# Cross-covariance attention on one core: one late store cut as 68 and 60 partitions, and all work in a new order

## The chip, the cores and the metric

The kernel runs on one core of a Trainium2 chip. The metric is the device time of one execution in microseconds; the other cores are idle. Beside it stands the span, the time from the first to the last instruction of the program in a profiled execution.

## The reference

```
Q, K, V: [8, 12, 512, 64] float32
Q_norm = Q / (norm(Q, axis=-2) + 1e-10)          # over the 512 positions
K_norm = K / (norm(K, axis=-2) + 1e-10)
attn = einsum('bhnd,bhne->bhde', Q_norm, K_norm)  # 64 x 64 for each head
attn = softmax(attn, axis=-1)                     # + 1e-10 under the line
out  = einsum('bhnd,bhde->bhne', V, attn)         # float32
```

There are 96 heads. Each of Q, K, V and the output is 12.58 MB.

## The kernel before, in words

The 96 heads are taken in twelve groups of eight, `s` = 0 to 11. Heads lie along partitions: a group's Q is one tile of 128 partitions by 2 x 1024 elements, 1 MB, and K is another. V comes in twelve loads of 1 MB, two for each pair of groups (`w` = 0 to 5); a group's output leaves as one store of 1 MB. So the program moves 48 times 1 MB: 24 loads of Q and K, 12 loads of V, 12 stores. The tiles of group 0 alone come in halves. Each 1 MB of Q, K or output consists of 256 rows of 4096 bytes, each row one DMA packet.

For a group: `cast_qk` makes bf16 copies of Q and K, `square` squares both, `grams` multiplies K by Q for each head (64 matmuls), `sums` adds the squares over the positions (8 matmuls), `fold`, `norms` and `powers` make the factors, `scale_k`, `logits`, `scales_q`, `exps` and `normalise` make the softmax. For a pair of groups `cast_v` casts V in four pieces, `vtrans` transposes it in four or five pieces, `vcopy` brings these out of PSUM. Then `outs` (16 matmuls) and `ocopy` run four times for each group, and `store` sends the group out.

Casts, squares and the copies out of PSUM may run on several engines. Which engine takes which piece, and the order of everything, is decided at build time by the planner `Order`: it steps through a list of pieces with costs (given where the pieces are added), ranks (`R`), preferences of engines (`BIAS`) and paces of the loads (`QK_PACE`, `V_FROM`, `V_PACE`, `ST_LAG`), always taking the piece that can begin first. The instructions are then emitted in that order, and each engine works through its own in order. So the constants in `PAR` fix the program.

All DMAs but two are issued by SyncE, in one queue. A DMA carries one of eight semaphores in turn, so it waits for the landing of the DMA eight before it; it waits too for its buffer. The numbers of buffers are in `PAR['NB']`: `qk` of Q and K tiles, `v` of V tiles, `sq` of squares, `so` of output tiles. `ocopy` of a group waits until the store that last used its `so` buffer has landed.

`store` sends a group in one DMA, except group 9 (`S - SPLIT`): it goes in two halves (`r` = 0, 1), each 128 rows of 4096 bytes, one a partition, and each half is cut along the partitions as `CUTS` says. Before, half 0 goes as partitions 0 to 85, 85 to 117 and 117 to 128, and half 1 whole. Groups 10 and 11 follow whole; they are the last two DMAs.

SyncE's order before (Q1 is the Q of group 1, V0 the first load of V, S0 the store of group 0):

```
Q0a Q0b | Q1 K1 V0 V1 Q2 K2 V2 Q3 K3 Q4 K4 V3 Q5 V4 K5 V5 Q6 K6 Q7 K7 V6 Q8 K8 V7 V8 Q9 K9
Q10 K10 V9 Q11 K11 S0 V10 V11 S1 S2 S3 S4 S5 S6 S7 S8 S9(85) S9(32) S9(11) S9(half 1) S10 S11
```

Of the kernel before, what the change touches and what calls it, by code (L numbers as in the profile page):

```python
# [10 lines left out]
AF = mybir.ActivationFunctionType  # L11
ALU = mybir.AluOpType

PAR = {'NB': {'qk': 7, 'v': 3, 'vb': 2, 'qm': 2, 'sq': 2, 'vt': 2, 'so': 6, 'sm': 2, 'ab': 4},
 'TAIL': 3,
 'FINE': (0,),
 'ACTQ': True,
 'X': 1.27,
 'R': {'ck': 14.3601,
       'q': -46.9145,  # L20
       'sq': -4.5261,
       'sk': 21.309,
       'gr': 31.9137,
       's1': -8.269,
       'rd': 14.1273,
       'nn': -13.565,
       'pw': -22.1669,
       'kx': 16.8281,
       'lg': -36.3133,
       'qs': 14.727,  # L30
       'ex': 7.4539,
       'nm': 23.5766,
       'cv': -5.1919,
       'vt': 13.5707,
       'vc': 31.4911,
       'ou': -17.6156,
       'oc': 6.4318},
 'BIAS': {('cv', 'DVE'): 12.3272,
          ('vc', 'ACT'): 5.2627,
          ('oc', 'DVE'): 7.9654,  # L40
          ('q0', 'ACT'): -9.0842,
          ('sk', 'ACT'): 4.174,
          ('sk', 'DVE'): 5.4091,
          ('cv', 'ACT'): 0.906,
          ('cv', 'POOL'): -0.1651,
          ('ck', 'DVE'): -11.8527,
          ('ck', 'ACT'): -10.4645,
          ('ck', 'POOL'): -15.4937,
          ('oc', 'ACT'): 4.7795,
          ('sq', 'DVE'): -12.3114,  # L50
          ('sq', 'ACT'): -21.9953,
          ('q0', 'DVE'): -28.6804,
          ('q0', 'POOL'): -29.3142,
          ('vc', 'DVE'): -20.4676},
 'QK_PACE': 0.9356,
 'V_FROM': 0.0874,
 'V_PACE': 0.7666,
 'ST_LAG': 6.0835,
 'SPLIT': 3,
 'CUTS': (((0, 85), (85, 117), (117, 128)), ((0, 128),))}  # L60

D = 64
T = 32
# [86 lines left out]
def kernel(  # L150
# [11 lines left out]
    W = S // 2  # L162
    TAIL = PAR["TAIL"]
    FINE = PAR["FINE"]

# [6 lines left out]

    NB = PAR["NB"]
    edge = ctx.enter_context(tc.tile_pool(name="edge", bufs=1))
# [25 lines left out]
    def cols(c):  # L200
        return slice(0, T) if c is None else slice(c * TT, (c + 1) * TT)
# [9 lines left out]
    def load_qk(s, x, c):  # L211
        w, e = divmod(s, 2)
        if (s, x) not in qk32:
            qk32[s, x] = qp.tile([128, T, D], F32, name="qk32")
        issue = nc.scalar if (s, x) == (0, 1) and PAR["ACTQ"] else nc.sync
        o = qk32[s, x][:, cols(c)].rearrange("p t d -> p (t d)")
# [10 lines left out]
    def store(s, i):  # L227
        if s == S - PAR["SPLIT"]:
            for r in range(2):
                o, y = Of[s // 2, s % 2, :, r], so[s][:, r].rearrange("p j d -> p (j d)")  # L230
                for a, b in PAR["CUTS"][r]:
                    nc.sync.dma_start(out=o[a:b], in_=y[a:b])
        elif i is None:
            nc.sync.dma_start(out=Of[s // 2, s % 2], in_=so[s].rearrange("p r j d -> p r (j d)"))
        else:
            nc.sync.dma_start(out=Of[s // 2, s % 2, :, i], in_=so[s][:, i].rearrange("p j d -> p (j d)"))
# [280 lines left out]
```

## Time and profile before

| | |
|---|---|
| time, median of 3 runs | 129.66 us (129.61 to 130.15) |
| time of the profiled execution | 129.72 us |
| its span | 127.6 us |
| bytes moved | 50.59 MB, 37.75 MB read and 12.58 MB written in HBM |
| busy: PE, DVE, ACT, POOL | 80.8, 80.4, 85.1, 47.0 us |
| granted TensorE clock, mean | 0.878 |

In the profile's rows PE is TensorE's matmuls, PEld its weight loads, DVE, ACT and POOL are VectorE, ScalarE and GpSimd; SPq is the queue of SyncE, which issues the DMAs. "DMA share" is the mean busy share of the core's 16 DMA engines; it can come out a little over 1. L12 is line 12 of the kernel. The profiled execution's time lies 2.1 us over its span.

### The profile page before, as it was taken

How to read it: one execution, taken by the hardware profiler on the slowest of the kernel's cores; microseconds unless marked ns; L12 is line 12 of the kernel's file. 1: busy time of each engine (PE TensorE's matmuls, PEld its weight loads, DVE VectorE, ACT ScalarE, POOL GpSimd, SP SyncE). 2: the span in 40 equal slices, each digit the busy share in tenths (PEclk: the TensorE clock that was granted, in tenths of full speed). 3: DMA queues.
4: the chain of work that ended last, by engine and by line, in shares of the span. 5: the costliest groups of instructions: out<-in, count | busy, mean ns of one | idle time of the engine just before them, and what ended most of it. 6: DMA issues, size and time to landing. Idle time of an engine off the chain costs nothing.

```text
span 127.6 us, 4062 instructions
## 1 busy us (share of the span) xinstructions
PE 80.8 (63%) x1800; PEld 54.0 (42%) x1800; DVE 80.4 (63%) x140; ACT 85.1 (67%) x116; POOL 47.0 (37%) x40
## 2 busy tenths in 40 slices
PE   0009459883797687676469897946999699950000
PEld 0006146560674365354336655532577267630000
DVE  2223344899836988889886699985699976600000
ACT  4076658794698826998798988839479757880000
POOL 3250665460545196054518805442516400000000
PEclk9999999999559999999976999995599967998555
DMA  4999999999999999999999999999999999999950
GB/s 117 412 419 437 421 414 437 408 420 416 429 420 429 419 420 408 421 415 428 407 434 415 416 419 420 428 414 416 430 419 416 414 417 414 415 416 406 408 234 15
DMA packets 11601, 50.59 MB, mean 396 GB/s; under 512 B 832, under 2 KB 832, under 8 KB 10048
## 3 DMA queue, kind: packets, MB, share of 16 engines
q1 hardware_dynamic: 11296, 49.29, 94.2%
q10 hardware_dynamic: 288, 1.05, 2.1%
q8 instruction: 14, 0.23, 0.6%
q14 instruction: 3, 0.02, 0.0%
HBM read 37.75 MB, written 12.58 MB: 394 GB/s over the span
## 4 chain that ended last, share of the span: by engine, by line
DMA 53%; PE 13%; DVE 12%; ACT 7%; SPq 4%; issue 2%
DMA qk<-in_Q_dram 36%; DMA v<-in_V_dram 17%; ACT so L205 4%; PE po L338 3%; SPq L225 3%; PE gram L289 3%; PE vps L323 3%; DVE ab L310 2%; PE l L266 2%; DVE vt L207 2%; PE gram L260 1%; DVE s L271 1%; ACT sq L251 1%; DVE sq L253 1%; ACT vb L205 1%
## 5 line engine op out<-in xcount | busy, mean ns | idle before, releaser
L209 POOL TENSOR_SCALAR kb<-qk 128x2048 bf16<-128x2048 f32 (+1 forms) x13 | 23.7, 1820 | 37.8 <-DMA qk<-in_K_dram 30.0
L251 ACT ACTIVATE sq<-qb 128x2048 bf16<-128x2048 bf16 (+1 forms) x13 | 23.1, 1778 | 8.2 <-DVE qb L207 8.2
L205 ACT COPY so<-po 128x512 f32<-128x512 f32 x47 | 25.6, 584 | 4.1 <-PE po L338 2.6
L209 POOL TENSOR_SCALAR vb<-v 128x1024 bf16<-128x1024 f32 x15 | 20.3, 1372 | 13.5 <-DMA v<-in_V_dram 9.8
L338 PE MATMUL po<-ab,vt 128*32 128x128 bf16 x768 | 20.6, 237 | 5.2 <-DVE ab L310 2.5
L260 PE MATMUL gram<-qb,kb 32*128 32x128 bf16 x768 | 15.3, 238 | 12.7 <-POOL kb L209 10.1
L323 PE MATMUL vps<-ident,vb 128*128 128x128 f32 x96 | 17.2, 304 | 4.9 <-POOL vb L209 2.7
L207 DVE CAST qb<-qk 128x2048 bf16<-128x2048 f32 (+1 forms) x12 | 13.6, 1137 | 10.3 <-DMA qk<-in_Q_dram 9.5
L266 PE MATMUL l<-sq,hm 128*32 128x512 bf16 x96 | 18.5, 446 | 2.1 <-ACT sq L251 1.5
L260 PEld LDWEIGHTS <-kb 32*128 32x128 bf16 x768 | 13.1, 104 | 14.8 <-POOL kb L209 11.4
L338 PEld LDWEIGHTS <-vt 128*32 128x32 bf16 x768 | 14.4, 103 | 11.2 <-issue 6.5
L207 DVE COPY vt<-vps 128x1024 bf16<-128x1024 bf16 (+1 forms) x25 | 16.5, 665 | 3.0 <-PE vps L323 2.7
L251 ACT ACTIVATE sq<-kb 128x2048 bf16<-128x2048 bf16 (+1 forms) x10 | 17.4, 1737 | 0.6 <-POOL kb L209 0.6
L205 ACT CAST vb<-v 128x1024 bf16<-128x1024 f32 x9 | 12.0, 1338 | 6.8 <-DMA v<-in_V_dram 6.8
L323 PEld LDWEIGHTS vps<-ident,vb 128*128 128x128 f32 x96 | 11.1, 151 | 8.7 <-POOL vb L209 3.3
L271 DVE TENSOR_REDUCE s<-l 64x128 f32<-64x512 f32 x12 | 8.1, 678 | 7.9 <-PE l L266 7.9
L289 PE MATMUL gram<-ident,kqs 128*128 128x128 f32 x48 | 9.7, 335 | 4.0 <-DVE kqs L285 3.7
L295 DVE TENSOR_TENSOR ls<-gram,r 64x256 f32<-64x256 f32 x24 | 10.1, 420 | 2.7 <-PE gram L289 2.3
L310 DVE TENSOR_TENSOR ab<-ex,rb 128x512 bf16<-128x512 f32 x12 | 10.4, 867 | 0.4
L285 DVE TENSOR_TENSOR kqs<-gram,r 128x512 f32<-128x512 f32 x12 | 8.3, 688 | 3.4 <-ACT r L281 2.9
L289 PEld LDWEIGHTS gram<-ident,kqs 128*128 128x128 f32 x48 | 6.2, 166 | 8.1 <-DVE kqs L285 7.3
L266 PEld LDWEIGHTS <-hm 128*32 128x32 bf16 x96 | 5.5, 104 | 9.4 <-issue 7.5
(25 smaller groups left out, 41.3 us busy)
## 6 DMA issues: line engine op xcount, KB each, us to landing
v<-in_V_dram SPq DMA_DIRECT2D x12, 1024.0 KB, 19.5
qk<-in_Q_dram SPq DMA_DIRECT2D x11, 1024.0 KB, 19.7
qk<-in_K_dram SPq DMA_DIRECT2D x11, 1024.0 KB, 19.7
out_dram<-so SPq DMA_DIRECT2D x11, 1024.0 KB, 15.3
qk<-in_K_dram ACTq DMA_DIRECT2D x2, 512.0 KB, 7.2
qk<-in_Q_dram SPq DMA_DIRECT2D x2, 512.0 KB, 5.8
out_dram<-so SPq DMA_DIRECT2D x1, 512.0 KB, 9.8
out_dram<-so SPq DMA_DIRECT2D x1, 340.0 KB
```

The source lines that it names most:

```text
L205: nc.scalar.copy(o, i)
L207: nc.vector.tensor_copy(o, i)
L209: nc.gpsimd.tensor_scalar(out=o, in0=i, scalar1=1.0, scalar2=0.0, op0=ALU.mult, op1=ALU.add)
L251: nc.scalar.activation(o, i, AF.Square)
L260: nc.tensor.matmul(gram[s][:, h, 0], k, q, start=(t == 0), stop=(t == TT - 1))
L266: nc.tensor.matmul(st[s][32 * x:32 * (x + 1)].rearrange("p t d -> p (t d)"), hm, sq[s][:, x, t:t + 4].rearrange("p t r d -> p (t r d)"), s ...
L271: nc.vector.tensor_reduce(out=s2[s], in_=st[s].rearrange("p t d -> p d t"), axis=mybir.AxisListType.X, op=ALU.add)
L289: nc.tensor.transpose(gram[s][:, h, 1], kqs[s][:, h], ident)
L295: nc.vector.tensor_tensor(out=ls[s][half], in0=gram[s][half, :, 1, half], in1=r12[s][half, :HU, None].to_broadcast([D, HU, D]), op=ALU.mult)
L310: nc.vector.tensor_tensor(out=ab[s], in0=ex[s][:, :, None, :].to_broadcast([128, HU, 2, D]), in1=rb[:, :, :, None].to_broadcast([128, HU, ...
L323: nc.tensor.transpose(ps[:, n], vb[w][:, j].rearrange("p r d c -> p (r d c)").bitcast(F32), ident)
L338: nc.tensor.matmul(po[s, x][32 * h:32 * (h + 1), j].rearrange("p r d -> p (r d)"), v, ab[s][:, h].rearrange("p r d -> p (r d)"), start=Tru ...
```

## The change

Only the constants in `PAR` change. One output buffer more (`so` 7), one buffer of squares less (`sq` 1), half 0 of group 9 cut in two pieces instead of three, and new ranks, preferences and paces for the planner, so that every engine's order is another.

```diff
-PAR = {'NB': {'qk': 7, 'v': 3, 'vb': 2, 'qm': 2, 'sq': 2, 'vt': 2, 'so': 6, 'sm': 2, 'ab': 4},
+PAR = {'NB': {'qk': 7, 'v': 3, 'vb': 2, 'qm': 2, 'sq': 1, 'vt': 2, 'so': 7, 'sm': 2, 'ab': 4},
...
- 'R': {'ck': 14.3601,
-       'q': -46.9145,
...
+ 'R': {'ck': 0.7103,
+       'q': 38.8577,
...
- 'BIAS': {('cv', 'DVE'): 12.3272,
...
+ 'BIAS': {('cv', 'DVE'): 4.9235,
...
- 'QK_PACE': 0.9356,
- 'V_FROM': 0.0874,
- 'V_PACE': 0.7666,
- 'ST_LAG': 6.0835,
+ 'QK_PACE': 2.1101,
+ 'V_FROM': 0.1602,
+ 'V_PACE': 1.9081,
+ 'ST_LAG': 7.2153,
  'SPLIT': 3,
- 'CUTS': (((0, 85), (85, 117), (117, 128)), ((0, 128),))}
+ 'CUTS': (((0, 68), (68, 128)), ((0, 128),))}
```

SyncE's order after:

```
Q0a Q0b | V0 Q1 K1 V1 Q2 K2 V2 Q3 K3 V3 Q4 K4 Q5 V4 K5 Q6 V5 K6 Q7 V6 K7 Q8 K8 V7 Q9 K9 V8
Q10 V9 K10 Q11 K11 S0 V10 S1 V11 S2 S3 S4 S5 S6 S7 S8 S9(68) S9(60) S9(half 1) S10 S11
```

The pieces that go to other engines, in numbers of instructions (whole tiles of 128 x 2048 unless said otherwise):

| | before | after |
|---|---|---|
| casts of Q and K on DVE / ACT / POOL | 10 / 0 / 12 | 4 / 11 / 7 |
| the same, half tiles of group 0 | 2 / 0 / 2 | 0 / 2 / 2 |
| squares on DVE / ACT | 3 / 19 | 10 / 12 |
| the same, half tiles | 0 / 4 | 3 / 1 |
| copies `so<-po` on DVE / ACT | 1 / 47 | 9 / 39 |
| half copies `vt<-vps` on DVE / ACT | 2 / 0 | 1 / 1 |
| casts of V on ACT / POOL | 9 / 15 | 9 / 15 |

On PE the numbers are the same. In the new order two more `outs` stand ahead of the first transpose of the last pair's V (12 come behind it instead of 14), and behind the `grams` of group 11 come 14 `outs` instead of 18.

More of the change, by code (lines that the diff above doesn't have):

```diff
@@ L18 @@
  'X': 1.27,
- 'R': {'ck': 14.3601,
-       'q': -46.9145,
[L21 to L37, printed above, removed]
- 'BIAS': {('cv', 'DVE'): 12.3272,
[L39 to L54, printed above, removed]
- 'QK_PACE': 0.9356,
- 'V_FROM': 0.0874,
- 'V_PACE': 0.7666,
- 'ST_LAG': 6.0835,
+ 'R': {'ck': 0.7103,
+       'q': 38.8577,
+       'sq': 30.5609,
+       'sk': 12.6274,
+       'gr': -25.7525,
+       's1': -14.196,
+       'rd': -7.9807,
+       'nn': -28.1345,
+       'pw': 11.9875,
+       'kx': -10.0108,
+       'lg': 26.5601,
+       'qs': -70.1832,
+       'ex': -6.0087,
+       'nm': 5.7641,
+       'cv': 31.9974,
+       'vt': 2.1204,
+       'vc': 5.5239,
+       'ou': 45.783,
+       'oc': -3.2712},
+ 'BIAS': {('cv', 'DVE'): 4.9235,
+          ('vc', 'ACT'): -0.5494,
+          ('oc', 'DVE'): -2.7787,
+          ('q0', 'ACT'): 2.8681,
+          ('sk', 'ACT'): -2.9801,
+          ('vc', 'DVE'): -1.2695,
+          ('oc', 'ACT'): -3.2943,
+          ('q0', 'DVE'): 2.5176,
+          ('q0', 'POOL'): 1.8248,
+          ('cv', 'ACT'): 3.3357,
+          ('cv', 'POOL'): 2.5761,
+          ('sq', 'DVE'): 8.6489,
+          ('sq', 'ACT'): 9.3919,
+          ('ck', 'DVE'): 19.4897,
+          ('ck', 'ACT'): -4.4523,
+          ('ck', 'POOL'): -4.7611,
+          ('sk', 'DVE'): -2.8832},
+ 'QK_PACE': 2.1101,
+ 'V_FROM': 0.1602,
+ 'V_PACE': 1.9081,
+ 'ST_LAG': 7.2153,
  'SPLIT': 3,
- 'CUTS': (((0, 85), (85, 117), (117, 128)), ((0, 128),))}
+ 'CUTS': (((0, 68), (68, 128)), ((0, 128),))}
 D = 64
```

## The prediction

> **What bounds the kernel now.** I read the page first: busy times, slices, DMA queues, chain.
>
> ```profile
> span 127.6 us, 4062 instructions
> PE 80.8 (63%) x1800; PEld 54.0 (42%) x1800; DVE 80.4 (63%) x140; ACT 85.1 (67%) x116; POOL 47.0 (37%) x40
> DMA  4999999999999999999999999999999999999950
> GB/s 117 412 419 437 421 414 437 408 420 416 429 420 429 419 420 408 421 415 428 407 434 415 416 419 420 428 414 416 430 419 416 414 417 414 415 416 406 408 234 15
> DMA packets 11601, 50.59 MB, mean 396 GB/s; under 512 B 832, under 2 KB 832, under 8 KB 10048
> q8 instruction: 14, 0.23, 0.6%
> DMA 53%; PE 13%; DVE 12%; ACT 7%; SPq 4%; issue 2%
> ```
>
> No compute engine is busy for more than 67% of the span, while the DMA engines are at 9 tenths or more from the second slice to the 38th, at 406 to 437 GB/s. So the transfers bound the kernel, and the bytes don't change. Only three things can move the time: a hole in the stream, its start, or its end. The start has the same first four DMAs (the halves of group 0). For the end I asked the windows of the last microseconds, in halves.
>
> ```profile
> core 0: us, PE busy (x), PEclk, DMA share, GB/s
> 120.00:121.00 1.00, 0.00 (x0) 0.50 0.98 401
> 121.00:121.50 0.50, 0.00 (x0) 0.50 0.80 328
> 121.50:122.00 0.50, 0.00 (x0) 0.50 0.90 369
> 122.00:122.50 0.50, 0.00 (x0) 0.50 0.70 287
> 122.50:123.00 0.50, 0.00 (x0) 0.50 0.68 279
> 123.00:123.50 0.50, 0.00 (x0) 0.50 0.58 238
> 123.50:124.00 0.50, 0.00 (x0) 0.50 0.18 74
> 124.00:124.50 0.50, 0.00 (x0) 0.50 0.18 74
> 124.50:125.00 0.50, 0.00 (x0) 0.50 0.06 25
> 125.00:125.50 0.50, 0.00 (x0) 0.50 0.06 25
> 125.50:126.00 0.50, 0.00 (x0) 0.50 0.06 25
> 126.00:126.50 0.50, 0.00 (x0) 0.50 0.02 8
> ```
>
> One of 16 engines is a share of 0.06. So the 16 don't end together: about nine work until 123.5, three until 124.5, and a single one, at 25 GB/s, until 126.1 or so. PE does nothing in these rows: the end is this one DMA engine. The shares from 121 on add up to 4.22 x 0.5 = 2.1 us of all engines. Spread evenly the work would be done at 123.1, so an ideal split is worth 3.0 us and no more. How the stores are dealt out is what counts.
>
> **What the last engine carries.** The timeline gives the issue of each late store, the DMA view its time to landing; I asked for them one by one.
>
> ```profile
> 106.97 0.37 SPq L234 DMA_DIRECT2D out_dram<-so  x1
> out_dram<-so SPq DMA_DIRECT2D x1, 1024.0 KB, 10.5
> out_dram<-so SPq DMA_DIRECT2D x1, 340.0 KB
> 110.34 0.34 SPq L232 DMA_DIRECT2D out_dram<-so  x1
> out_dram<-so SPq DMA_DIRECT2D x1, 128.0 KB, 9.9
> 111.83 0.36 SPq L232 DMA_DIRECT2D out_dram<-so  x1
> out_dram<-so SPq DMA_DIRECT2D x1, 512.0 KB, 9.8
> 114.89 0.38 SPq L234 DMA_DIRECT2D out_dram<-so  x1
> out_dram<-so SPq DMA_DIRECT2D x1, 1024.0 KB, 11.7
> ```
>
> A store has landed when its slowest engine is through. The store ahead of the cut one landed at 106.97 + 10.5 = 117.5, the 32 partitions at 120.2, half 1 at 121.6, the last store at 126.6. From half 1 to the end are two stores, 32 rows of 4096 bytes for each engine, in 5.0 us: 0.155 us a row. Half 1 with its 8 rows takes 1.25 us of the 1.4 before it, and one more row is left, of the 11 partitions. From 117.5 to 120.2 are 2.7 us, 17.5 rows; two are of the 32 partitions (32/16), so some 15 to 17 are of the 85. Dealt evenly, 85 rows would be 5.3 for each engine. The last engine thus carries 16 of them: about five engines carry them all, and the view has no landing for this store, as it has for the evenly dealt ones. In sum this engine takes 17 + 2 + 1 = 20 rows where an uncut half would give it 8, 12 x 0.155 = 1.9 us more, and it was among the slowest already. It is alone for the last 1.6 us.
>
> **The cut, costed.** The bounds for the 68 and the 60: dealt evenly, 4.25 and 3.75 rows an engine, 8 in all; dealt as the 85, with 17 rows on each of four engines, 17 and about 4. So the last engine has 21 rows after, if it is one of the four: +1 row, +0.16 us (+0.3 with 22). If it is the fifth, it has 4 instead of 20: -16 rows, -2.5 us, and the next engines, until now through at 124.5, set the end with +0.16: 124.7 for 126.1, -1.4 us. Dealt evenly, it has 12 less, -1.9 us; five engines' relief falls on the other eleven, 12 x 5/11 = 5.5 rows or 0.85 us, and those that now end at 123.5 end at 124.4: -1.7 us. I take 17 and 4, since the row is nearest to that, and the last engine as one of the four, 4 to 1. Three DMAs become two: SyncE issues one less (0.34 us), hidden, as it waits for copies there.
>
> The Trainium skill, "DMA: Bandwidth & Descriptors", section on why a DMA increments its semaphore by 16, states the rule: the number of engines is the largest up to 16 that divides the outermost size, and the lowest-numbered ones are taken. By it 85 goes to five engines, 68 to four and 60 to fifteen, the fifth engine is left with 4 rows, and the sum would be the same two cases; the trace's 16 rows agree. Its rule for kernel authors on two transfers to disjoint partition halves says that both spray over all 16 engines; by that one the balance would come out even at -1.7 us, and this trace speaks against it.
>
> **The new order, costed.** It matters only where a DMA would be late, so its cover comes first.
>
> ```profile
> DMA to landing us min/median/max: 9.0/19.7/21.2
> 97.61 2.62 POOL L209 TENSOR_SCALAR vb<-v 128x1024 bf16<-128x1024 f32 x2 [1.11 <-DMA v<-in_V_dram]
> 100.12 2.17 ACT L205 COPY so<-po 128x512 f32<-128x512 f32 x4 [0.85 <-PE l L266]
> L251 ACT ACTIVATE sq<-qb 128x2048 bf16<-128x2048 bf16 x11 | 21.0, 1909 | 4.3 <-DVE qb L207 4.3
> L209 POOL TENSOR_SCALAR kb<-qk 128x2048 bf16<-128x2048 f32 x11 | 20.9, 1901 | 32.6 <-DMA qk<-in_K_dram 24.8 <-PE gram L289 3.1 <-PE l L266 3.1
> L207 DVE CAST qb<-qk 128x2048 bf16<-128x2048 f32 x10 | 12.3, 1226 | 5.0 <-DMA qk<-in_Q_dram 4.2 <-PE po L338 0.7
> L205 ACT CAST vb<-v 128x1024 bf16<-128x1024 f32 x9 | 12.0, 1338 | 6.8 <-DMA v<-in_V_dram 6.8
> L253 DVE TENSOR_TENSOR sq<-kb 128x2048 bf16<-128x2048 bf16 x3 | 4.9, 1629 | 0.1
> L207 DVE COPY so<-po 128x512 f32<-128x512 f32 x1 | 0.7, 673 | 0.0
> L205 ACT COPY so<-po 128x512 f32<-128x512 f32 x47 | 25.6, 584 | 4.1 <-PE po L338 2.6 <-PE l L266 0.9
> L266 PE MATMUL l<-sq,hm 128*32 128x512 bf16 x96 | 18.5, 446 | 2.1 <-ACT sq L251 1.5 <-DVE sq L253 0.5
> ```
>
> The first row is of the loads of Q and K: a median of 19.7 us from issue to landing, at 2.5 us for 1 MB (32 x 0.155 / 2), is eight transfers deep. SyncE waits for the DMA eight before far more than for a buffer; a cast that is late by some microseconds is hidden. At the end the last store is issued at 114.9 and lands 11.7 us later, of which its own 16 rows are 2.5. For the last engine the cover is 9 us; for the first to run dry (share under 1 from 121 on, less 2.5) it is 3.6 us, and a delay there falls on engines with time to spare.
>
> Work moved. DVE: -6 casts x 1.226, -2 halves at 0.7 (half of it and the fixed part), +8 copies x 0.673, +7 squares x 1.629, +3 halves at half of that, -1 half copy: -7.4 - 1.4 + 5.4 + 11.4 + 2.4 - 0.4 = +10 us, 90 busy. ACT: -7 squares x 1.909, -3 halves, -8 copies x 0.584, and 11 casts and 2 halves that it didn't do before, between its square's 1.9 and two V casts' 2.7 each: +2 to +12 us, 87 to 97 busy; I take 88, as a square reads and writes the same layout as this cast. POOL: -5 x 1.9, 37 busy. All stay below the 115 us until the last store's issue.
>
> `sq` 2 to 1: a group's squares wait for the sums before (18.5/12 = 1.5 us on PE), then take 1.9 on two engines side by side: 3.5 us a group against the 5 us in which its Q and K land. Nothing, unless PE's order puts the sums late. `so` 6 to 7: the copies in the ACT row at 100.12 need the landing of the store six groups back, and may have waited 0.85 us for it; after, a group's copies wait for a store that lies one earlier in the queue. That gains cover. V: the last load lands one transfer, 2.5 us, later. Its two casts, both on POOL before (2.62), are one on POOL and one on ACT after, -1.3; and two `outs` fewer, some 0.6 us of copies each, are behind it: 2.5 - 1.3 - 1.2 = 0. S0 now stands ahead of V10 in SyncE's queue and S1 ahead of V11: were the copies of group 1 late, V11 would be issued late, and its casts and the last transposes wait for it. But the `outs` of group 1 are ahead of the `grams` of group 4 in PE's order, long before. The new order costs nothing under this cover; without it each microsecond beyond 9 is one of the time.
>
> **Sum.** Profiled execution 129.72, + 0.16 for the row, 0 for the rest: 129.9; against the median, 0.06 lower, and with the 15 to 17 rows read for 17 taken as they are, 129.7 to 129.9. I say 129.7. About 0.5% (0.65 us) is what a measurement of this kernel can tell from no change.
>
> **Rivals.** (1) The last engine is relieved: it is the fifth, or its lag has another cause than the engine itself and falls elsewhere in the new order. For: its lag before the cut is no part of the cut, and one in five by count. Against: nothing in the rows names the cause. Time: 129.66 - 1.4 = 128.2. The skill's rule on the lowest-numbered engines allows it only for the fifth.
>
> (2) The lag on a loaded engine grows. The 14 packets of the q8 row take 0.006 x 16 x 127.6 / 14 = 0.87 us of one engine each, as 5 to 6 rows; PE's instructions are the same in number, but one such packet that falls on the last engine after the new order is + 0.9: 129.7 + 0.2 + 0.9 = 130.8. It decides from + 4 rows on (0.65 us). For: the cut leaves 17 rows on four engines and no slack there.
>
> (3) Compute is late. In-order queues on DVE at 90 us and ACT at up to 97 put the last store's issue from 114.9 to beyond 124, 9 us later; at 11 us it is 129.7 + 2 = 131.7. Against: 25 us of idle ACT, and fewer `outs` at the end.
>
> **How the numbers follow.** Forecast 0.46, (1) 0.30, (2) 0.14, (3) 0.10. Over 0.5% faster is (1) 0.30; within it the forecast 0.46; slower (2) and (3) 0.24. The range takes in (1) and (2): 128.0 to 130.8; the forecast's own is 129.2 to 130.2.
>
> **What would show it.** Right: in the last windows one to four engines alone (0.06 to 0.25) for 1.5 us or more, the last stores landing about 5 us after half 1, their issue before 116. Rival (1): the share falls from 0.5 to 0 within 1 us, at 125 or earlier. (2): one engine alone for over 2 us. (3): a share under 0.9 before 120, and a store issued after 120. The step would be wrong if the landing of the 60 partitions came under 2 us after that of the store ahead: the 17 rows would not be on the slowest engine.

## The result

The changed kernel takes 128.38 us (median of 16 runs), the kernel before 129.74 us in the same series: ratio 0.9898, 95% interval 0.9878 to 0.9918. It is 1.0% or 1.3 us faster; 129.7 was forecast, and the time lies where the first rival put it (128.2). Three of the 16 runs, at 133.0 to 134.3 us, were in a slower state that executions of this program fall into now and then; the ratios here and below leave such runs out. The profiled execution of the changed kernel took 129.28 us, 0.9 us above its median, so its page shows the kernel at its longer end.

The page after, the same lines as before:

```profile
span 127.2 us, 4071 instructions
PE 79.0 (62%) x1800; PEld 52.5 (41%) x1800; DVE 86.3 (68%) x149; ACT 88.0 (69%) x112; POOL 39.5 (31%) x35
DMA  3999999999999999999999999999999999999970
GB/s 90 394 438 407 438 411 424 419 422 426 412 424 424 416 422 420 408 426 419 416 429 410 431 411 428 412 419 428 415 428 417 415 419 412 417 413 407 415 305 21
q8 instruction: 14, 0.23, 0.6%
```

The stream is as dense as it was, 394 GB/s in the second slice and 407 to 438 from there, and slice 39 now moves 305 GB/s instead of 234. DVE is 6 us busier, which changes nothing in the stream. The difference is in the last microseconds, here in the same windows:

```profile
120.00:121.00 1.00, 0.00 (x0) 0.50 1.04 426
121.00:121.50 0.50, 0.00 (x0) 0.50 0.90 369
121.50:122.00 0.50, 0.00 (x0) 0.50 0.78 320
122.00:122.50 0.50, 0.00 (x0) 0.50 0.80 328
122.50:123.00 0.50, 0.00 (x0) 0.50 0.76 311
123.00:123.50 0.50, 0.00 (x0) 0.50 0.72 295
123.50:124.00 0.50, 0.00 (x0) 0.50 0.54 221
124.00:124.50 0.50, 0.00 (x0) 0.50 0.14 57
124.50:125.00 0.50, 0.00 (x0) 0.50 0.10 41
125.00:125.50 0.50, 0.00 (x0) 0.50 0.08 33
125.50:126.00 0.50, 0.00 (x0) 0.50 0.02 8
```

Eight or nine of 16 engines work until 124, against three before; a single one is left at 125.5, and its last packet ends at 125.8, 0.4 us earlier than before even in this long execution.

### The profile page after: what moved, and what is told of

It is laid out like the page before. It is cut to its first block, busy times and chain, and to the rows that moved or that the text cites. A ratio compares the mean times of both kernels' runs of the same rounds, so it can differ in the third digit from the quotient of the medians.

```text
span 127.2 us, 4071 instructions
## 1 busy us (share of the span) xinstructions
PE 79.0 (62%) x1800; PEld 52.5 (41%) x1800; DVE 86.3 (68%) x149; ACT 88.0 (69%) x112; POOL 39.5 (31%) x35
## 4 chain that ended last, share of the span: by engine, by line
DMA 37%; DVE 22%; PE 15%; ACT 9%; issue 4%; SPq 2%; ACTq 0%; DVEq 0%
DMA qk<-in_K_dram 37%; PE l L266 6%; PE gram L260 4%; DVE sq L253 4%; ACT so L205 4%; DVE ls L295 3%; DVE vt L207 3%; DVE kqs L285 3%; SPq L225 2%; PE gram L289 2%; ACT kb L205 2%; DVE ab L310 2%; DVE qb L207 2%; PE vps L323 2%; PE po L338 2%
## 5 line engine op out<-in xcount | busy, mean ns | idle before, releaser
L209 POOL TENSOR_SCALAR vb<-v 128x1024 bf16<-128x1024 f32 x15 | 22.9, 1546 | 42.4 <-DMA v<-in_V_dram 32.9
L260 PE MATMUL gram<-qb,kb 32*128 32x128 bf16 x768 | 16.8, 251 | 13.4 <-ACT kb L205 9.9
L205 ACT COPY so<-po 128x512 f32<-128x512 f32 x39 | 21.7, 582 | 4.6 <-PE po L338 4.4
L205 ACT CAST kb<-qk 128x2048 bf16<-128x2048 f32 (+1 forms) x10 | 17.3, 1728 | 8.7 <-DMA qk<-in_K_dram 8.3
L260 PEld LDWEIGHTS <-kb 32*128 32x128 bf16 x768 | 14.4, 112 | 16.2 <-ACT kb L205 12.1
L251 ACT ACTIVATE sq<-kb 128x2048 bf16<-128x2048 bf16 (+1 forms) x10 | 18.2, 1825 | 3.0 <-PE l L266 1.8
L338 PEld LDWEIGHTS <-vt 128*32 128x32 bf16 x768 | 13.2, 100 | 12.3 <-issue 7.5
L253 DVE TENSOR_TENSOR sq<-qb 128x2048 bf16<-128x2048 bf16 (+1 forms) x10 | 12.1, 1205 | 5.9 <-POOL qb L209 5.9
L209 POOL TENSOR_SCALAR qb<-qk 128x2048 bf16<-128x2048 f32 (+1 forms) x6 | 9.7, 1613 | 12.0 <-DMA qk<-in_Q_dram 6.7
L289 PE MATMUL gram<-ident,kqs 128*128 128x128 f32 x48 | 8.8, 310 | 6.4 <-DVE kqs L285 6.4
## 6 DMA issues: line engine op xcount, KB each, us to landing
qk<-in_K_dram SPq DMA_DIRECT2D x11, 1024.0 KB, 19.7
```

Of the source, the lines that this page charges most:

```text
L205: nc.scalar.copy(o, i)
L209: nc.gpsimd.tensor_scalar(out=o, in0=i, scalar1=1.0, scalar2=0.0, op0=ALU.mult, op1=ALU.add)
L251: nc.scalar.activation(o, i, AF.Square)
L253: nc.vector.tensor_tensor(out=o, in0=i, in1=i, op=ALU.mult)
L260: nc.tensor.matmul(gram[s][:, h, 0], k, q, start=(t == 0), stop=(t == TT - 1))
L289: nc.tensor.transpose(gram[s][:, h, 1], kqs[s][:, h], ident)
```

## The experiments

Two theories. **F**: the last engine before was the fifth of those that carried the 85 partitions; the new cut leaves it 4 rows in place of 20. **L**: the lag that the last engine gathers ahead of the cut is smaller in the new order, and the cut adds only a row. The first four kernels separate the cut from the order.

**Cut alone.** The order of before with `'CUTS': (((0, 68), (68, 128)), ((0, 128),))`.

> The order of before with the new cut (68 and 60). Theory F (the last engine was the fifth of those that carried the 85 partitions, and the new cut takes 16 rows from it): all of the gain, 128.3 us, the share of the DMA engines falling to 0 by 125 us of the span. Theory L (the lag that the last engine gathers before the cut is smaller in the new order; the cut itself only adds a row of 0.155 us): 129.8 us, one engine alone to 126 us as before.

Measured: 128.25 us, ratio 0.9868 (0.9826 to 0.9911). The cut by itself brings all of the gain.

**Order alone.** The changed kernel with the old cut.

```diff
- 'CUTS': (((0, 68), (68, 128)), ((0, 128),))}
+ 'CUTS': (((0, 85), (85, 117), (117, 128)), ((0, 128),))}
```

> The new order with the old cut (85, 32 and 11). Theory F: no gain, 129.7 us. Theory L: all of the gain and one row more, 128.2 us.

Measured: 129.48 us, ratio 0.997 (0.9941 to 0.9998). The whole new order, the two buffers included, is worth 0.3% (0.02 to 0.59%), and not the 1.2% that L asks for. L falls. The windows of the cut alone (profiled at 128.75 us, 0.5 over its median) and then those of the order alone:

```profile
123.50:124.00 0.50, 0.00 (x0) 0.50 0.29 115
124.00:124.50 0.50, 0.00 (x0) 0.50 0.10 41
124.50:125.00 0.50, 0.00 (x0) 0.50 0.06 25
125.00:125.50 0.50, 0.00 (x0) 0.50 0.02 8
```

```profile
123.50:124.00 0.50, 0.00 (x0) 0.50 0.18 74
124.00:124.50 0.50, 0.00 (x0) 0.50 0.18 74
124.50:125.00 0.50, 0.00 (x0) 0.50 0.08 33
125.00:125.50 0.50, 0.00 (x0) 0.50 0.06 25
125.50:126.00 0.50, 0.00 (x0) 0.50 0.02 8
```

With the old cut the lone engine stands in either order; with the new cut, in the order of before, the last one is through at 125.2.

That the 17 rows are not on the engine that is slowest ahead of the cut is read from the landings too. The timeline and the DMA view of the cut alone, for the store ahead of the cut, the 60 partitions and the last store:

```profile
106.77 0.37 SPq L234 DMA_DIRECT2D out_dram<-so  x1
out_dram<-so SPq DMA_DIRECT2D x1, 1024.0 KB, 10.6
109.96 0.34 SPq L232 DMA_DIRECT2D out_dram<-so  x1
out_dram<-so SPq DMA_DIRECT2D x1, 240.0 KB, 9.3
114.75 0.38 SPq L234 DMA_DIRECT2D out_dram<-so  x1
out_dram<-so SPq DMA_DIRECT2D x1, 1024.0 KB, 10.8
```

The slowest engine is through the store ahead at 117.4 and all engines through the 60 partitions at 119.3: 1.9 us, where 17 + 4 rows on the slowest one would take 21 x 0.155 = 3.3. This is the test that the prediction named: under 2 us the 17 rows are not on the slowest engine. The same lines of the changed kernel give 117.7 and 119.9, 2.2 us: over the 2 us named, but still well under 3.3.

```profile
105.11 0.38 SPq L234 DMA_DIRECT2D out_dram<-so  x1
out_dram<-so SPq DMA_DIRECT2D x1, 1024.0 KB, 12.6
111.68 0.34 SPq L232 DMA_DIRECT2D out_dram<-so  x1
out_dram<-so SPq DMA_DIRECT2D x1, 240.0 KB, 8.2
```

The test does not say which engine the late one was. The packets do, followed as described further below: in the kernel before, the last engine, known by a lag that it gathers store by store, carried 17 of the 85 rows; in the profile of the cut alone the engine with that lag has only 4 rows, of the 60, and ends at 123.5 instead of 126.2.

**The half left whole**, in the order of before and in the new one.

```diff
+ 'CUTS': (((0, 128),), ((0, 128),))}
```

> The order of before, the half left whole as 128 partitions: 8 rows for each engine in place of 20 on the five. Both theories: the last engine ends 12 rows earlier, 1.9 us; the others get 5 to 6 rows more, 0.85 us, and those that ended at 123.5 to 124 of the span end at 124.4 to 124.9: 128.0 to 128.5 us. If the lag belongs to no particular engine (theory N: whichever engine gets the uneven rows falls behind), the same. If the 85 rows were dealt evenly in spite of the landings read from them: 129.7.

> The new order, the half left whole. Theory F: four engines have 13 rows less, twelve have 4 to 8 more (0.6 to 1.2 us); the twelve set the end: 128.4 to 129.0 us. Theory L: the last engine is one of the four that carry 17 rows and ends 2.0 us earlier, so the others set the end: 127.7 to 128.6 us.

Measured: 128.26 us (0.987, 0.9832 to 0.9908) and 128.18 us (0.9859, 0.9813 to 0.9906). The second lies under F's 128.4 to 129.0 and within L's 127.7 to 128.6. It does not bring L back, which the order alone speaks against; F's working for this case put the other engines too late. The changed kernel gains nothing over no cut at all: what it undoes is the harm of the old one. The windows of the first of these:

```profile
122.50:123.00 0.50, 0.00 (x0) 0.50 0.54 221
123.00:123.50 0.50, 0.00 (x0) 0.50 0.42 172
123.50:124.00 0.50, 0.00 (x0) 0.50 0.46 188
124.00:124.50 0.50, 0.00 (x0) 0.50 0.42 172
124.50:125.00 0.50, 0.00 (x0) 0.50 0.05 16
```

Seven engines (0.44 x 16) end together, at 124.3 to 124.7, and nine have ended by 123. There is no lone one.

**Three pieces, but even**, against the reading that the number of stores cost time.

```diff
+ 'CUTS': (((0, 80), (80, 112), (112, 128)), ((0, 128),))}
```

> The order of before, half 0 in three pieces again, but of 80, 32 and 16 partitions, which are dealt evenly over 16 engines: 5 + 2 + 1 = 8 rows each. Theory F (uneven rows on the fifth engine cost the time): 128.25 us, as the uncut half. If the number of stores cost it: 129.7.

Measured: 128.28 us (0.9883, 0.9868 to 0.9897). So it is not the number of stores that costs time, but how their rows are dealt.

**More on the five.**

```diff
+ 'CUTS': (((0, 95), (95, 128)), ((0, 128),))}
```

> The order of before, half 0 as 95 and 33 partitions. If 95 rows go to five engines, 19 each, and 33 to eleven, 3 each, the first five engines have 22 rows in place of 20. Theory F: the last engine ends two rows, 0.31 us, later: 130.05 us. If the 95 partitions are dealt in another way, 129 us or less.

Measured: 130.43 us, ratio 1.0044 (1.003 to 1.0058): slower, as F says, by 0.57 us (0.39 to 0.75) where two rows are 0.31. The way is right, the size is not. By its packets the fifth engine came to the cut at 117.0 us here, against 116.7 in the kernel before, 0.3 us later, which is of the size of the rest; why it did stays open. The lone engine now lasts until 126.6:

```profile
125.00:125.50 0.50, 0.00 (x0) 0.50 0.06 25
125.50:126.00 0.50, 0.00 (x0) 0.50 0.06 25
126.00:126.50 0.50, 0.00 (x0) 0.50 0.08 33
```

**Why the fifth engine is late.** The trace holds every DMA packet, but not which engine it is on. An engine's packets follow each other without gaps, so the small packet with which an engine reports a store comes 2.490 us after that of the store before, and the 16 engines can be followed by it. What a store takes over 2.490 us, in ns, for the nine stores S0 to S8, worked out from the packets of the kernel before (the last figure of the first row has an instruction packet of 8 KB, 309 ns, in it):

```
fifth of the five   -1  136  503  184  235  343  357  417  556
another of the five -1    0    1    0    1    0    1    0    1
```

It loses 2.7 us over S1 to S8, 2.4 without that packet, and nothing over the loads. The engine counts agree: each engine reports once, and the 85 partitions were reported 5 times, the 68 4 times, the 60 15 times. PE then runs through many short instructions, `outs` among them; S0, where it lost nothing, passed this engine from 86.7 to 89.1 us, and the windows of before show 11 matmuls in the 5 us around that, against 128 from 95 to 100, where S2 passed it:

```profile
85.00:90.00 5.00, 2.68 (x11) 1.26 (x12) 3.11 (x5) 4.85 (x6) 1.79 (x1) 0.61 1.03 418
95.00:100.00 5.00, 4.95 (x128) 3.05 (x117) 4.79 (x9) 4.27 (x5) 3.73 (x3) 1.00 1.02 411
```

So a kernel with fewer of PE's instructions, and all else kept (the matmul of four heads in one):

```diff
-            for h in range(HU):
-                x16 = slice(16 * (4 * half + h), 16 * (4 * half + h + 1))
-                v = vt[w][:, 4 * x + j, x16, :].rearrange("p x c -> p (x c)")
-                nc.tensor.matmul(po[s, x][32 * h:32 * (h + 1), j].rearrange("p r d -> p (r d)"), v,
-                                 ab[s][:, h].rearrange("p r d -> p (r d)"), start=True, stop=True, tile_position=(0, 32 * h))
+            v = vt[w][:, 4 * x + j, 64 * half:64 * (half + 1), :].rearrange("p x c -> p (x c)")
+            nc.tensor.matmul(po[s, x][:, j].rearrange("p r d -> p (r d)"), v,
+                             ab[s][:, 0].rearrange("p r d -> p (r d)"), start=True, stop=True)
```

> The order and the cut of before, but outs does one matmul of 128 columns for four heads in place of four of 32, with the first head's softmax for all four: a quarter of these weight loads and matmuls, 384 in place of 1536, with wrong outputs. Loads, copies and stores are unchanged. What makes the fifth engine late while it stores? Theory P (the instructions that PE runs through at that time): the lag is mostly gone, 128.2 us or less. Theory S (storing alone): 129.7 us. There are fewer 16 KB instruction packets, about 10 for 14, but the fifth engine shows none of them.

Measured: 128.32 us (0.9893, 0.9876 to 0.9911), with the old cut. From its packets, the same nine stores (the last figure with the 8 KB packet again):

```
fifth of the five    1    1  281  113  103  136  126   70  576
```

The lag over S1 to S8 is 1.4 us instead of 2.7 (1.1 instead of 2.4 without that packet). This speaks for theory P, that PE's instructions make the lag, and not for more than that: the late stores also left 2.4 to 2.8 us earlier, about half of the lag remains, and why an engine that stores should feel PE's instructions, and only this one, no run shows. Its page has 9 packets of 16 KB where there were 14.

```profile
q8 instruction: 9, 0.15, 0.4%
```

**A better cut.** A quarter of the columns of half 0 whole, the rest as 68 and 60 partitions, in the order of before:

```diff
-                for a, b in PAR["CUTS"][r]:
-                    nc.sync.dma_start(out=o[a:b], in_=y[a:b])
+                for a, b, c, d in PAR["CUTS"][r]:
+                    nc.sync.dma_start(out=o[a:b, c:d], in_=y[a:b, c:d])
...
+ 'CUTS': (((0, 68, 0, 768), (68, 128, 0, 768), (0, 128, 768, 1024)), ((0, 128, 0, 1024),))}
```

> The order of before; half 0 with 768 of its 1024 columns cut as 68 and 60 partitions, and the last 256 columns whole. In rows of 4096 bytes the first four engines have 0.75 x 21 + 0.25 x 8 = 17.75, the next eleven 5, the last one 2. Against the uncut half (eight engines last at 124.7 to 125.1 of the span, four of the first at 121.8 to 122.8) the late ones gain 3 rows, 0.47 us, and the first four lose 9.75, 1.5 us, to 124.4 at most: 127.8 us, 0.4 us under the uncut half. If pieces of 3 KB and 1 KB cost more than their bytes: 128.2 or more.

Measured: 127.84 us, ratio 0.985 (0.9835 to 0.9865). It beats both kernels; the working was right. Its windows:

```profile
123.00:123.50 0.50, 0.00 (x0) 0.50 0.60 246
123.50:124.00 0.50, 0.00 (x0) 0.50 0.44 180
124.00:124.50 0.50, 0.00 (x0) 0.50 0.03 8
```

> The new order with the mixed cut: 768 columns of half 0 as 68 and 60 partitions, the last 256 columns whole. If the order matters little once the fifth engine is spared, the same time as with the order of before, 127.8 us; if the new order is worth something of its own (the two orders with the old cut differ by 0.3 us), 127.5 us.

Measured for the same cut in the new order: 127.81 us, ratio 0.9849 (0.983 to 0.9867). The orders are level.

**The changed kernel again.**

> The changed kernel once more, unchanged, for a profile of another execution: 128.4 us. Its profiled execution took 129.28 us, 0.9 us over its median, with a lone engine until 125.5 us. If that engine is one of the four with 17 rows and was held up by chance, this execution ends by 125.0 us of the span, with all engines through within 1 us of each other from half of them on; if the lone engine belongs to the kernel, it is there again.

Measured: 128.25 us (0.9903, 0.9881 to 0.9925), but the profiled execution was again a long one, 128.84 us, with one engine from 124.5 to 125.4:

```profile
124.00:124.50 0.50, 0.00 (x0) 0.50 0.22 90
124.50:125.00 0.50, 0.00 (x0) 0.50 0.06 25
125.00:125.50 0.50, 0.00 (x0) 0.50 0.04 16
```

In both profiles of the changed kernel, then, one engine is late, and both are of executions above the median. For the first of them the packets tell which it is, since the engines can be told by their rows: not the fifth, which ended at 123.7, but one of the four with 17 rows, which ended at 125.8; the other three ended at 123.9, 123.9 and 124.9. It needed 4.6 us for its 17 + 4 rows, where 21 x 0.155 are 3.3, because six of its packets, between 116.7 and 119.6 us, lasted 0.30 to 0.44 us instead of 0.16. The cut alone, profiled in a long execution too, shows the same: the engine that ends at 125.2 is one of the four, with six such packets (0.29 to 0.40 us) between 116.3 and 119.0. No instruction packet lies on these engines there, and PE had run its last matmul before 115 us in both, so this delay is neither that of the 16 KB packets nor of PE's instructions; its cause stays open. In the profile of 128.84 us many engines have slow packets from 114 to 118.5 us, and the last one can't be told. Whether the runs at 128.2 have such a delay can't be seen, since they were not profiled.

## Why the prediction was wrong

- **What bounds the kernel: right.** The stream is full in every kernel run, and the end moves as the late rows are dealt out: 128.3 dealt evenly, 129.7 with 20 rows on five engines, 130.4 with 22.
- **What the last engine carries: right.** 16 of 85 rows, about five engines, were read from three landings. By the packets it had 17. That the reading came so near is in part luck: the engine whose landing at 117.5 it starts from is another one, 0.4 us later than the last engine there. The trace has five reports for the 85 partitions and four for the 68. The Trainium skill's rule ("DMA: Bandwidth & Descriptors", why a DMA increments its semaphore by 16) gives these counts. The Trainium skill's rule for kernel authors on disjoint partition halves (same page), that both spray over all 16, doesn't hold for these pieces: the half whole or evenly cut is 1.5 us faster than the uneven one.
- **The cut, costed: the step that failed** is "the last engine as one of the four, 4 to 1". I counted engines as if each were as likely to be last. It was the fifth: with the old order and the new cut the time falls to 128.25 us, and by the packets the engine with the lag then has 4 rows and ends among the others. The sum for that case was right in size: -1.4 us said, -1.5 measured for the cut alone (129.77 to 128.25). The landings can say how many rows the last engine has but not which one it is, and the sum hung on just that; so the choice of 4 to 1 had no row to rest on.
- **The new order at nothing: right.** Order alone 0.997 (0.9941 to 0.9998), and with the mixed cut both orders at 127.8. The cover held: loads are in flight 19.8 us in the median, 19.7 before. (S0 stood ahead of V10 in SyncE's queue before too; only S1 ahead of V11 is new.) The sizes were near: DVE 86 us busy for 90 said, ACT 88 for 88, POOL 39.5 for 37. The row that I chose for ACT's casts was the right one, the squares on DVE came out shorter than the row of before:

```profile
DMA to landing us min/median/max: 11.2/19.8/21.0
L205 ACT CAST kb<-qk 128x2048 bf16<-128x2048 f32 x8 | 15.2, 1898 | 3.9 <-DMA qk<-in_K_dram 3.5 <-PE gram L260 0.4
L253 DVE TENSOR_TENSOR sq<-qb 128x2048 bf16<-128x2048 bf16 x8 | 10.7, 1334 | 0.0
```

- **The rivals.** (1) came true in its first form, the fifth engine; its second form, that the lag falls elsewhere in a new order, didn't: with the old cut the lone engine was there in the new order too. (2) shows in part in the long executions: one of the four engines with 17 rows was held up by 1.3 us in the changed kernel's profile, though not by an instruction packet, and the time with it was 129.28 us, not 130.8. (3) was never near: the last store was issued at 115.3 us of the span, against 114.9 in the kernel before.

- **The signs.** Read alone, the changed kernel's page looks like the forecast: one or two engines alone from 124.0 to 125.8 us, the last store issued before 116, and a time of 129.28 us within the forecast's own 129.2 to 130.2. But it is a page of a long execution, and the engine that it shows is late for another reason than the forecast gave. The median of the runs and the cut alone decide, not the page.

## What to carry to other kernels

In a kernel that fills the DMA engines from start to end, look at the last five microseconds engine by engine: the area under the DMA share says what an even end is worth, and a share of 1/16 is one engine's debt. The number of partitions in a store sets how many engines it goes to (here 85 went to 5, 68 to 4, 60 to 15), so a cut is a way to shift work between engines, for good or ill; compare it first with the store left whole. When a forecast hangs on which of several alike engines is the late one, test that on the chip ahead of all else, with the one-line change that spares one of them.

## What the runs showed of the hardware

One of 16 DMA engines lost 0.14 to 0.50 us with each of eight stores of 1 MB in the kernel before, while PE for most of that time ran through short matmuls, and nothing with loads; a quarter of the `outs` instructions took the sum from 2.4 to 1.1 us, without the 0.31 us of an 8 KB instruction packet in each. And each 16 KB instruction packet held up one engine by 1.3 to 1.4 us, more than the 0.9 us that it lasts, as the two packets of data behind it are slow (0.44 and 0.25 to 0.36 us instead of 0.16). The 14 of them fall on eight engines in turn, so six are hit twice; with the half left whole, these six and the fifth engine are the seven that end last. In two long executions one engine lost 1.1 to 1.3 us over six slow packets after PE's last matmul, for a cause that no run shows.
